# Moving gate products between three stages of a hybrid encoder block, with one convolution tap on ScalarE

## The chip, the cores and the metric

The kernel runs on one core of a Trainium2 chip. The time is that of the device in microseconds (us), median of repeated runs; a profile comes from one further execution. PE is TensorE (matmul), PEld its weight load, DVE VectorE, ACT ScalarE, POOL GpSimd, SP the queue that issues most DMAs.

## The reference

One layer of an encoder block over 1024 tokens of width 1024, in float32.

```python
h = rms_norm(x, norm1_w[l]) * (1.0 + scale1) + shift1
proj = h @ w_in[l]
q, k, v, xBC, z, dt_raw, gates = jnp.split(proj, offsets, axis=-1)
...
attn = block_attention(q, k, v)                    # 16 query heads of 64, 4 key/value heads, softmax over all tokens
ssd = ssd_mixer(xBC, z, dt_raw, ...)               # centred convolution of 5 taps, SiLU, chunked scan in both directions
g_attn = jax.nn.sigmoid(gates[..., :D_MODEL])
g_ssd = jax.nn.sigmoid(gates[..., D_MODEL:])
merged = g_attn * (attn @ w_attn_out[l]) + g_ssd * (ssd @ w_ssd_out[l])
x = x + gate1 * (merged @ w_o[l])
...
ff = jnp.square(jax.nn.relu(h2 @ w_mlp1[l])) @ w_mlp2[l]
x = x + gate2 * ff
```

The gates are 2048 columns of the input projection, 16 chunks of 128 columns. They are needed only after the scan, when the two branches are merged. The convolved columns xBC are 24 chunks.

## The kernel before

Every float32 matrix product is done as three: each operand is split into a high part (a cast on ACT) and a low part (a subtraction on DVE or POOL), and high x high, high x low and low x high are summed in PSUM. The function `split` at lines 168 to 170 does both steps, so all low parts are recorded under line 155 and all high casts under line 169.

The stages follow one another: modulation and norm; the projections for q, k, v and z; the convolved pairs (lines 704 to 843); attention (848 to 974); the scan (995 to 1206); the merge and the rest.

In the **convolved pairs** two chunks of 128 columns are projected together by seven block products instead of eight (a Winograd form of Strassen's scheme). The loop at line 802 goes over `pairs`. A pair loads its weights as `r0` and `r1` (`load_pair`; `r1` has one buffer), POOL forms four sums of weight blocks (`w_sum`), each product (`product`, 12 matmuls of 512 columns) takes an operand from one of four slots (`w1_op`), and DVE and POOL add the products into two padded rows `pa` and `pb`. For a convolved pair `conv` then runs five taps over each padded row: the first by a tensor_scalar on DVE at line 712, four more by scalar_tensor_tensor at 715, and SiLU on ACT at 717. Two pairs later at most, `to_tokens` turns the result by 16 transposes per pair. A gate pair is only written out. `GPOS` says at which places of the list gate pairs stand; with `(13,)` one gate pair stands last, and `GATES` = 14 chunks remain for direct products.

In **attention** a unit `u` is 128 queries of one head, 128 units in all: `scores(u)` (four matmuls), a maximum on DVE (line 893), the exponential on ACT (895), `turn` (eight transposes, then a split), and for each four units `values`, 16 matmuls. The sums of the exponentials are collected in `zall` and inverted only at the end (lines 965 to 969). Direct gate products run beside it: `weave` (line 64) takes the next step of the stream whose declared cost used so far is the smaller share of its declared total, so PE's order is written out by hand (`manual_schedule(engines=M2)`), 12 chunks at 10.4 beside 128 units at 2.72. A chunk is 2 halves of 24 matmuls. The other engines' order and the DMA queues' order are made by the planner from its own estimate of time.

In the **scan** the same weave runs `scan` beside `products`: the two remaining gate chunks, the attention's output product (8 chunks, with `load_a` reading outputs and reciprocals back, multiplying them on DVE and splitting them), and, once `pipe["done"]` has reached 16 scan chunks, the scan's output product. The tiles of the normed input `h` and of the read-back outputs `a` share one pool of 32 tiles (tag "act").

Of the kernel before, what the change touches and what calls it, by code (L numbers as in the profile page):

```python
# [9 lines left out]
F32 = mybir.dt.float32  # L10
# [8 lines left out]
P = 128  # L19
# [14 lines left out]
QKV_N = 400  # L34
GATES_EARLY = 12
LEAD2 = 0
# [7 lines left out]
NPRE = 5  # L44
GPOS = (13,)
KR = 4
# [45 lines left out]
def block(ctx: ExitStack, tc: tile.TileContext, ia, out, upto=99, dbg=None):  # L92
# [97 lines left out]

    def gemm_cm(ps_pool, tag, wsrcs, ahi, alo, evac, bufs=None, pair=False, then=None, e_lo=None):

        ws = {0: load_w(wsrcs[0], e_lo=e_lo)}
        if then:
            then()
        n = len(wsrcs)
        order = [(i, h) for i in range(n) for h in range(2)]
        if pair:
            order[:4] = [(0, 0), (1, 0), (0, 1), (1, 1)]
        for i, half in order:  # L200
            if half == 0 and i + 1 < n and i + 1 not in ws:
                ws[i + 1] = load_w(wsrcs[i + 1], e_lo=e_lo)
            hi, lo = ws[i]
            if 1:
                ps = ps_pool.tile([P, 512], F32, name=tag, tag=tag, bufs=bufs)
                for k in range(KT):
                    T.matmul(ps, hi[:, k], ahi[k][half], start=k == 0, stop=False)  # L207
                    T.matmul(ps, hi[:, k], alo[k][half], start=False, stop=False)  # L208
# [495 lines left out]
    with tc.tile_pool(name="p2", bufs=1, reuse_waits="tile") as p2, \  # L704
# [5 lines left out]
        def conv(i, pad):  # L710
            acc = accs.pop() if accs else acc_tile()
            V.tensor_scalar(out=acc, in0=pad[:, 0:S], scalar1=cwT[:, i:i + 1], scalar2=vecT[:, CB0 + i:CB0 + i + 1],
                            op0=ALU.mult, op1=ALU.add)
            for k in range(1, 5):
# [133 lines left out]
    with tc.tile_pool(name="p3k", bufs=1, reuse_waits="tile") as p3k, \  # L848
# [3 lines left out]
        def gates_stream(pool, psp, i0, i1, bufs=2, e_lo=None):  # L852
# [5 lines left out]
            yield from gemm_cm(psp, "psg", [w_cols(w_in, OFF_G + i * P) for i in range(i0, i1)], hhi, hlo, evac, bufs=bufs, e_lo=e_lo)  # L858

        def attn_stream():  # L860

# [47 lines left out]

            pvs = {}  # L910

            def values(b, hf):

                h = b // 2
                v1 = kv[h // 4][2]
                if hf == 0:
                    pvs[b] = ps3.tile([P, 512], F32, name="pv", tag="pv", bufs=1)
                pv, ph, pl = pvs[b], phs.pop((b, hf)), pls.pop((b, hf))
# [9 lines left out]
                if hf == 1:  # L928
                    ax = p3.tile([HD, 512], F32, name="ax", tag="ax", bufs=1)
                    A.copy(ax, pv[HD:])  # L930
                    av = p3.tile([HD, 512], F32, name="av", tag="av", bufs=2)
                    tt(V, av, ax, pv[:HD], ALU.add)
                    dma(av_d[h // 2][(h % 2) * HD:(h % 2 + 1) * HD, (b % 2) * 512:(b % 2 + 1) * 512], av)
                yield 0.92

# [13 lines left out]
            for u in range(NU + 4):  # L949
# [13 lines left out]
                if u % 4 == 3 and u < NU:  # L963
                    pvq = all_values(u // 4)
            ps = ps3.tile([P, 4, P], F32, name="pst", tag="pst", bufs=2)
            T.transpose(ps[:, 0], zall, ident)
            zt = p3.tile([P, P], F32, name="zt", tag="pf", bufs=2)
            V.reciprocal(zt, ps[:, 0])
            dma(rz_d.rearrange("h (a b) -> (h a) b", b=P), zt)

        with tc.manual_schedule(engines=M2):
            weave(tc, (attn_stream(), 128 * 2.72 + L0), (gates_stream(p3, ps3, 0, GATES_EARLY, 1, G), GATES_EARLY * 10.4), lead=LEAD2)
    if upto <= 3:
        return dict(gt_d=gt_d, av_d=av_d, rz_d=rz_d)


    def out_stream(ps_pool, tag, wsrcs, hi, lo, dst, pool, then, bufs=2):
        def evac(i, half, ps):
# [3 lines left out]

        yield from gemm_cm(ps_pool, tag, wsrcs, hi, lo, evac, bufs=bufs, pair=True, then=then)

# [10 lines left out]
    with tc.tile_pool(name="p4", bufs=1, reuse_waits="tile") as p4, \  # L995
# [712 lines left out]
```

## Time and profile before

| | |
|---|---|
| median of 3 runs | 2608.29 us (2607.74 to 2609.0) |
| profiled execution, its own time | 2610.79 us |
| its span, first to last instruction | 2608.8 us |
| mean granted TensorE clock | 0.975 |
| busy: PE, PEld, DVE, ACT, POOL | 93%, 74%, 71%, 42%, 39% |

Busy shares are means over stages with different limits, so the stages are read one at a time. Matmuls are pipelined: the time of one is longer than the distance to the next, and the distance is what counts. In a row of waits stand: engine, tile and line that waited, what released it, total us, times, longest us. In a row of groups stand: line, engine, operation, tiles, shapes and count; then busy us and mean ns; then idle us before them and who ended it.

### The profile page before, as it was taken

The numbers are of one execution on the slowest core, as the hardware profiler recorded it, in microseconds if no ns is written. First come the engines' busy times: TensorE is split into PE (matmuls) and PEld (weight loads), VectorE is DVE, ScalarE is ACT, GpSimd is POOL, SyncE is SP. The second block draws the span as 40 slices with busy tenths as digits, with TensorE's granted clock in tenths as the row PEclk, the third lists the DMA queues.
The fourth block names the chain that finished last, engine by engine and source line by source line (L and its number), as shares of the span: only waits on it lengthen the run. The fifth ranks groups of instructions, "written<-read, shape, count | busy, mean of one in ns | idle before, by whom it ended". The sixth has DMA issues, their size and how long they took to land.

```text
span 2608.8 us, 32331 instructions
## 1 busy us (share of the span) xinstructions
PE 2435.3 (93%) x11340; PEld 1940.2 (74%) x11340; DVE 1844.4 (71%) x2200; ACT 1105.0 (42%) x1928; POOL 1016.0 (39%) x728
## 2 busy tenths in 40 slices
PE   5999999998989999999799999998989999899995
PEld 5998777776767777777567767776777888688884
DVE  5756347888856666666487787546569888768889
ACT  5455422333346666666233444343332222364441
POOL 2310117766710000000155666424018866633356
PEclk9999999999999999999899999999999999899998
DMA  7653741323441212111866675466315544754432
GB/s 258 184 157 124 253 152 61 89 85 93 145 140 45 77 45 79 47 52 29 239 216 196 194 223 169 125 221 207 133 49 178 189 144 144 265 179 149 142 93 97
DMA packets 286788, 369.69 MB, mean 142 GB/s; under 512 B 34201, under 2 KB 167041, under 8 KB 286625
## 3 DMA queue, kind: packets, MB, share of 16 engines
q1 hardware_dynamic: 215297, 292.62, 36.3%
q10 hardware_dynamic: 71328, 74.99, 8.7%
q8 instruction: 90, 1.47, 0.2%
q14 instruction: 73, 0.60, 0.1%
HBM read 251.33 MB, written 116.20 MB: 141 GB/s over the span
## 4 chain that ended last, share of the span: by engine, by line
PE 67%; DVE 11%; DMA 8%; issue 6%; POOL 5%; ACT 2%; SPq 1%; DVEq 0%; ACTq 0%; POOLq 0%
PE pst L906 5%; PE pp L1313 4%; PE pp L1315 4%; PE pp L1314 4%; PE psq L381 4%; PE psq L382 4%; PE psq L380 4%; PE psg L207 3%; PE psg L208 3%; PE psg L209 3%; PE p L1655 3%; PE p L1656 3%; PE p L1654 3%; PE pss L889 2%; PE pss L891 2%
## 5 line engine op out<-in xcount | busy, mean ns | idle before, releaser
L893 DVE TENSOR_REDUCE nm<-pss 128x1 f32<-128x1024 f32 x128 | 156.6, 1224 | 140.1 <-PE pss L891 139.6
L381 PE MATMUL psq<-twl,hh 128*128 128x400 f32 (+1 forms) x512 | 192.9, 378 | 5.9 <-DVE twl L155 4.1
L1655 PE MATMUL p<-o,o 128*128 128x512 f32 x448 | 179.8, 401 | 19.1 <-DVE o L155 19.1
L380 PE MATMUL psq<-twh,hh 128*128 128x400 f32 (+1 forms) x512 | 192.2, 381 | 3.7 <-ACT qkvr L513 1.2
L382 PE MATMUL psq<-twh,hl 128*128 128x400 f32 (+1 forms) x512 | 191.8, 377 | 0.0
L155 DVE TENSOR_TENSOR pl<-pst,ph 128x512 fp32r<-128x512 f32 x256 | 168.4, 684 | 27.5 <-ACT ph L169 27.5
L1654 PE MATMUL p<-o,o 128*128 128x512 f32 x448 | 177.3, 399 | 9.6 <-ACT o L169 7.7
L895 ACT ACTIVATE pf<-pss,nm 128x1024 f32<-128x1024 f32 x128 | 142.8, 1115 | 101.6 <-PE pst L906 98.0
L155 POOL TENSOR_TENSOR wlo<-wraw,whi 128x1024 fp32r<-128x1024 f32 x12 | 28.7, 2390 | 399.0 <-ACT whi L169 358.3
L1656 PE MATMUL p<-o,o 128*128 128x512 f32 x448 | 177.0, 397 | 0.0
L169 ACT CAST ph<-pst 128x512 fp32r<-128x512 f32 x256 | 146.3, 585 | 51.7 <-PE pst L906 37.5
L906 PEld LDWEIGHTS pst<-masks,pf 128*128 128x128 f32 x1024 | 118.8, 140 | 66.2 <-issue 28.8
L906 PE MATMUL pst<-masks,pf 128*128 128x128 f32 x1024 | 157.0, 276 | 9.7 <-DVE pl L155 9.6
L155 POOL TENSOR_TENSOR sl<-sl 128x512 f32<-128x512 f32 x64 | 95.0, 1492 | 175.5 <-DVE o L155 83.2
L715 DVE SCALAR_TENSOR_TENSOR cacc<-pad,cwT,cacc 128x1024 f32<-128x1024 f32 x96 | 149.7, 1570 | 0.4
L169 ACT CAST o<-ar 128x512 fp32r<-128x512 f32 x112 | 69.8, 623 | 175.8 <-PE p L1656 155.2
L155 DVE TENSOR_TENSOR o<-ar,o 128x512 fp32r<-128x512 f32 x112 | 107.2, 957 | 48.1 <-ACT o L169 48.1
L169 ACT CAST wop<-ws 128x512 fp32r<-128x512 f32 x116 | 70.6, 620 | 122.7 <-PE pp L1315 69.2
L1655 PEld LDWEIGHTS p<-o,o 128*128 128x128 f32 x448 | 86.5, 193 | 41.6 <-DVE o L155 23.7
L381 PEld LDWEIGHTS psq<-twl,hh 128*128 128x128 f32 x512 | 98.5, 192 | 17.9 <-DVE twl L155 5.2
L155 DVE TENSOR_TENSOR o<-sl,o 128x512 fp32r<-128x512 f32 x112 | 111.3, 994 | 0.1
L380 PEld LDWEIGHTS psq<-twh,hh 128*128 128x128 f32 x512 | 98.0, 192 | 16.0 <-ACT qkvr L513 1.7
(416 smaller groups left out, 7166.0 us busy)
## 6 DMA issues: line engine op xcount, KB each, us to landing
ar<-r SPq DMA_DIRECT2D x112, 256.0 KB
wada<-in_w_ada_dram SPq DMA_DIRECT2D x48, 512.0 KB
r<-in_w_mlp_dram SPq DMA_DIRECT2D x32, 512.0 KB
r<-as SPq DMA_DIRECT2D x64, 256.0 KB
sl<-in_w_mlp_dram SPq DMA_DIRECT2D x64, 256.0 KB
r<-in_w_in_dram SPq DMA_DIRECT2D x26, 512.0 KB
r<-ro ACTq DMA_DIRECT2D x48, 256.0 KB
xb<-cst ACTq DMA_DIRECT2D x20, 512.0 KB
```

The lines of the kernel that those rows point to most:

```text
L155: e.tensor_tensor(out=o, in0=a, in1=b, op=op)
L169: (e_hi or A.copy)(hi, src)
L380: T.matmul(o, hhi[k][half][:, sl], hi[:, k % 2, :n], start=k == 0, stop=False)
L381: T.matmul(o, hhi[k][half][:, sl], lo[:, k % 2, :n], start=False, stop=False)
L382: T.matmul(o, hlo[k][half][:, sl], hi[:, k % 2, :n], start=False, stop=k == KT - 1)
L715: V.scalar_tensor_tensor(out=acc, in0=pad[:, k:k + S], scalar=cwT[:, 24 * k + i:24 * k + i + 1], in1=acc, op0=ALU.mult, op1=ALU.add)
L893: V.tensor_reduce(out=nm, in_=ps, axis=AX.X, op=ALU.max, negate=True)
L895: A.activation(pfs[u], ps, AF.Exp, bias=nm, accum_out=zall[:, u:u + 1])
L906: T.transpose(pt[:, k], pf[:, (hf * 4 + k) * P:(hf * 4 + k + 1) * P], ident)
L1654: T.matmul(pss[t], a[:, 0, sl], b[:, 0], start=k == 0, stop=False)
L1655: T.matmul(pss[t], a[:, 0, sl], b[:, 1], start=False, stop=False)
L1656: T.matmul(pss[t], a[:, 1, sl], b[:, 0], start=False, stop=k == KR - 1)
```

## The change

- `GPOS` becomes `(2, 5, 8, 11, 16)`: five gate pairs stand among the 17 pairs; six chunks remain for direct products, all of them in attention, none in the scan.
- In `conv` the first tap is an activation (Identity with scale and bias) on ScalarE.
- In `values` the reciprocals of a block of four units are formed on DVE, written to DRAM element by element, and read back broadcast over 64 partitions; POOL multiplies the output with them before it is written.
- A new `load_a` inside attention's second stream, behind the gates, loads and splits the first two weight chunks of the attention's output product and reads the outputs back, each two heads as soon as they are written.
- In the scan the product starts with what was loaded; the old `load_a` and the division there go.

```diff
-GATES_EARLY = 12
-GPOS = (13,)
+GPOS = (2, 5, 8, 11, 16)
...
-            V.tensor_scalar(out=acc, in0=pad[:, 0:S], scalar1=cwT[:, i:i + 1], scalar2=vecT[:, CB0 + i:CB0 + i + 1],
-                            op0=ALU.mult, op1=ALU.add)
+            A.activation(acc, pad[:, 0:S], AF.Identity, scale=cwT[:, i:i + 1], bias=vecT[:, CB0 + i:CB0 + i + 1])
...
+        heads = [0]
+        w_ahead = {}
+
+        def load_a():
+
+            hi, lo = act_tiles("a", KT)
+            for i in range(2):
+                w_ahead[i] = load_w(w_cols(w_ao, i * P), e_lo=G)
+            yield 2
+            for k in range(KT):
+                while heads[0] < 2 * k + 2:
+                    yield None
+                for half in range(2):
+                    raw = p3.tile([P, 512], F32, name="araw", tag="araw", bufs=2)
+                    dma(raw, av_d[k][:, half * 512:(half + 1) * 512])
+                    split(hi[k][half], lo[k][half], raw, e_lo=G)
+                yield 2
+            w_ahead["a"] = hi, lo
+
+        def beside():
+            yield from gates_stream(p3, ps3, 0, GATES, 1, G)
+            yield from load_a()
+
...
                 if hf == 0:
+                    zi = p3.tile([P, 4], F32, name="zi", tag="zi", bufs=2)
+                    V.reciprocal(zi, zall[:, 4 * b:4 * b + 4])
+                    row = rz_d[h:h + 1, (b % 2) * 512:(b % 2 + 1) * 512]
+                    dma(row.rearrange("a (t p) -> p (a t)", p=P), zi)
+                    rzs[b] = p3.tile([HD, 512], F32, name="rz", tag="rz", bufs=2)
+                    dma(rzs[b], rz_d[h, (b % 2) * 512:(b % 2 + 1) * 512].partition_broadcast(HD))
...
                     tt(V, av, ax, pv[:HD], ALU.add)
+                    tt(G, av, av, rzs.pop(b), ALU.mult)
                     dma(av_d[h // 2][(h % 2) * HD:(h % 2 + 1) * HD, (b % 2) * 512:(b % 2 + 1) * 512], av)
+                    heads[0] = (b + 1) // 2
...
-            ps = ps3.tile([P, 4, P], F32, name="pst", tag="pst", bufs=2)
-            T.transpose(ps[:, 0], zall, ident)
-            zt = p3.tile([P, P], F32, name="zt", tag="pf", bufs=2)
-            V.reciprocal(zt, ps[:, 0])
-            dma(rz_d.rearrange("h (a b) -> (h a) b", b=P), zt)
...
-            weave(tc, (attn_stream(), 128 * 2.72 + L0), (gates_stream(p3, ps3, 0, GATES_EARLY, 1, G), GATES_EARLY * 10.4), lead=LEAD2)
+            weave(tc, (attn_stream(), 128 * 2.72 + L0), (beside(), GATES * 10.4 + 18), lead=LEAD2)
...
-        ahi, alo = act_tiles("a", KT)
-
-        def load_a():
-            for half in range(2):
-                ns = slice(half * 512, (half + 1) * 512)
-                for k in range(KT):
-                    raw = p4.tile([P, 512], F32, name="araw", tag="araw", bufs=3)
-                    dma(raw, av_d[k][:, ns])
-                    rz = p4.tile([P, 512], F32, name="rz", tag="rz", bufs=2)
-                    for j in range(2):
-                        dma(rz[j * HD:(j + 1) * HD, :], rz_d[2 * k + j, ns].partition_broadcast(HD))
-                    tt(V, raw, raw, rz, ALU.mult)
-                    split(ahi[k][half], alo[k][half], raw)
-
+        ahi, alo = w_ahead.pop("a")
...
-            yield from gates_stream(p4, ps4, GATES_EARLY, GATES)
-            yield from out_stream(ps4, "psg", [w_cols(w_ao, i * P) for i in range(KT)], ahi, alo, a_d, p4, load_a)
+            yield from out_stream(ps4, "psg", [w_cols(w_ao, i * P) for i in range(KT)], ahi, alo, a_d, p4, ws=w_ahead)
...
-            weave(tc, (scan(), 32 * (5.54 + YC) + SC0 + 7 * SC1), (products(), 166.4 + (GATES - GATES_EARLY - HELD) * 10.4), lead=LEAD3)
+            weave(tc, (scan(), 32 * (5.54 + YC) + SC0 + 7 * SC1), (products(), 166.4 - HELD * 10.4), lead=LEAD3)
```

More of the change, by code (lines that the diff above doesn't have):

```diff
@@ L189, in w_cols, with gemm_cm @@
         return w[k0 * P:(k0 + KT) * P, c0:c0 + P].rearrange("(k p) c -> p k c", p=P)
-    def gemm_cm(ps_pool, tag, wsrcs, ahi, alo, evac, bufs=None, pair=False, then=None, e_lo=None):
-        ws = {0: load_w(wsrcs[0], e_lo=e_lo)}
+    def gemm_cm(ps_pool, tag, wsrcs, ahi, alo, evac, bufs=None, pair=False, then=None, e_lo=None, ws=None):
+        ws = ws or {0: load_w(wsrcs[0], e_lo=e_lo)}
         if then:
@@ L908, in turn @@
                 split(phs[b, hf][:, :, js], pls[b, hf][:, :, js], pt)
-            pvs = {}
+            pvs, rzs = {}, {}
             def values(b, hf):
@@ L964, in attn_stream, with out_stream @@
                     pvq = all_values(u // 4)
-            ps = ps3.tile([P, 4, P], F32, name="pst", tag="pst", bufs=2)
-            T.transpose(ps[:, 0], zall, ident)
-            zt = p3.tile([P, P], F32, name="zt", tag="pf", bufs=2)
-            V.reciprocal(zt, ps[:, 0])
-            dma(rz_d.rearrange("h (a b) -> (h a) b", b=P), zt)
         with tc.manual_schedule(engines=M2):
-            weave(tc, (attn_stream(), 128 * 2.72 + L0), (gates_stream(p3, ps3, 0, GATES_EARLY, 1, G), GATES_EARLY * 10.4), lead=LEAD2)
+            weave(tc, (attn_stream(), 128 * 2.72 + L0), (beside(), GATES * 10.4 + 18), lead=LEAD2)
     if upto <= 3:
         return dict(gt_d=gt_d, av_d=av_d, rz_d=rz_d)
-    def out_stream(ps_pool, tag, wsrcs, hi, lo, dst, pool, then, bufs=2):
+    def out_stream(ps_pool, tag, wsrcs, hi, lo, dst, pool, then=None, bufs=2, ws=None):
         def evac(i, half, ps):
@@ L981, in evac @@
             adma(dst[i][:, half * 512:(half + 1) * 512], st)
-        yield from gemm_cm(ps_pool, tag, wsrcs, hi, lo, evac, bufs=bufs, pair=True, then=then)
+        yield from gemm_cm(ps_pool, tag, wsrcs, hi, lo, evac, bufs=bufs, pair=True, then=then, ws=ws)
     def load_g(pool, k0, hi, lo):
```

## The prediction

> **What bounds the kernel now.** I read the page first, then busy time by windows, then in each touched stage the waits, the groups of instructions and the order of time. The change touches three stages: the convolved pairs (414 to 732 us), attention (about 741 to 1246) and the scan (1246 to 1716). The windows list PE, PE weight load, DVE, ACT and POOL busy time, then granted clock, DMA share and GB/s.
>
> ```profile
> span 2608.8 us, 32331 instructions
> ...
> 492.10:516.80 24.70, 21.63 (x102) 17.16 (x101) 20.83 (x19) 8.95 (x15) 17.48 (x15) 1.00 0.30 86
> 709.30:732.20 22.90, 19.26 (x84) 14.95 (x82) 18.73 (x17) 7.05 (x9) 12.13 (x11) 1.00 0.81 268
> 760.00:1240.00 480.00, 472.76 (x2499) 362.11 (x2498) 324.39 (x402) 316.74 (x557) 28.59 (x18) 1.00 0.19 54
> 1220.00:1240.00 20.00, 19.05 (x104) 14.51 (x103) 12.94 (x18) 12.79 (x24) 4.40 (x7) 1.00 0.07 20
> 1290.00:1300.00 10.00, 5.72 (x11) 2.91 (x11) 4.21 (x6) 2.76 (x4) 2.16 (x2) 0.52 1.05 271
> 1420.00:1440.00 20.00, 20.00 (x91) 14.38 (x90) 16.25 (x18) 7.59 (x16) 13.04 (x11) 1.00 0.66 197
> ```
>
> Attention is bound by PE (98.5% busy), and so is the scan after its first 70 us. The convolved pairs are not: a convolved pair takes 24.7 us, of which PE works 21.63. The waits between 438 and 709 us say what it lacks, and a piece of the chain of work through one pair says why.
>
> ```profile
> PE psc L770 <- DVE wop L155: 20.3, 10, 2.3
> PE psc L770 <- POOL wop L155: 6.4, 6, 2.4
> DVE cacc L712 <- POOL pad L155: 24.5, 11, 2.3
> ```
>
> ```profile
> 572.59 1.40 DMA r<-in_w_in_dram
> ...
> 576.46 2.00 POOL ws L155
> ...
> 585.42 1.06 POOL pad L155
> 586.51 1.58 DVE cacc L712
> ...
> 590.23 0.67 DVE pad L155
> ...
> 596.63 0.61 DVE wop L155
> ...
> 597.30 1.40 DMA r<-in_w_in_dram
> ```
>
> This is a loop of 24.7 us: the weights land (3.9 us), POOL forms its sums and the pad add (10.0 us), DVE works off convolution taps (from 586.5 on), and only then splits the low part of the fifth operand (596.63 to 597.24). That frees the single buffer for the next load, and PE stands 2.03 us before it. What PE would need alone comes from the order of time:
>
> ```profile
> 563.16 0.39 PE L768 MATMUL psc<-hh,wop 128*128 128x512 f32 x1
> 565.88 0.39 PE L768 MATMUL psc<-u2h,wop 128*128 128x512 f32 x1
> 573.17 0.63 PE L768 MATMUL psc<-u4h,wop 128*128 128x512 f32 x1
> 573.60 0.63 PE L769 MATMUL psc<-u4l,wop 128*128 128x512 f32 x1
> 576.31 1.03 PE L732 MATMUL pst<-masks,cacc 128*128 128x128 f32 x8
> ```
>
> Twelve matmuls lie between the first two starts, so one takes 2.72/12 = 0.227 us (0.43 us behind the 2 us gap, where the clock is lower). A pair has 7 products of 12 matmuls, 19.05 us; two convolved chunks add 16 transposes, 2.06 us. PE's floor is 21.1 us for a convolved pair and 19.05 for a gate pair.
>
> **The change part by part.** *Matmuls.* A gate chunk done directly is 2 halves x 24 = 48 matmuls; a pair done in seven products is 84 instead of 96. Four pairs move: 336 matmuls (+76.2 us) come into the convolved pairs, 6 x 48 = 288 (65.4 us) leave attention and 96 (21.8 us) leave the scan: 48 matmuls, 10.9 us fewer. The rest is decided by stalls.
>
> *Convolved pairs.* The first tap leaves DVE:
>
> ```profile
> L712 DVE TENSOR_SCALAR cacc<-pad,cwT,vecT 128x1024 f32<-128x1024 f32 x22 | 35.8, 1627 | 24.5 <-POOL pad L155 24.5
> L155 DVE TENSOR_TENSOR wop<-r,wop 128x512 fp32r<-128x512 f32 x33 | 32.0, 973 | 14.7 <-ACT wop L169 14.7
> L717 ACT ACTIVATE cacc<-cacc 128x1024 f32<-128x1024 f32 x22 | 23.4, 1061 | 130.3 <-DVE cacc L715 130.3
> ```
>
> Two taps of 1.63 us leave the DVE stretch of the loop and one ACT pass of 1.06 us enters it ahead of the first remaining tap (price by the SiLU row, the same shape on the same engine): 24.7 - 3.26 + 1.06 = 22.5 us. Behind a gate pair DVE has no backlog and the pair comes near PE's 21.1. As six convolved pairs follow a convolved one and six a gate pair or the start, I take 21.9 on average; the ends are 21.1 (PE) and 24.7 (nothing gained). ACT's time is covered: 8.95 us busy of 24.7, and 2.1 more. A gate pair in the middle keeps 5 pad adds and 3 low splits on DVE, about 6.3 us, but inherits the taps in front of it; I take 20.0 (ends 19.05 and 22.9, the last gate pair now). Now: 12 x 24.7 + 21.5 = 318 us. After: 12 x 21.9 + 4 x 20.0 + 21.5 = 364. **+46 us**, ends +33 and +92.
>
> On the port the Trainium skill has a rule (SBUF — State Buffer, Who interferes with whom): a DVE instruction in a two-port mode, or with two SBUF inputs, and a GpSimd instruction reading SBUF lock each other out, and ScalarE never waits. The tap's 1.63 us would then be time taken from POOL as well, and the pairs would reach PE's floor, 10 us better; the sum keeps POOL's 10.0 us as measured.
>
> *Attention.* First the score tiles' instructions (count, least, median and longest ns, first and last start), then groups between 760 and 1240 us, PE's own wait there, and the third load of queries in SP's queue:
>
> ```profile
> L893 DVE TENSOR_REDUCE nm<-pss x128: 1214/1225/1226, 742.4 to 1230.9; 128x1 f32<-128x1024 f32 x128
> ...
> L895 ACT ACTIVATE pf<-pss,nm x128: 1113/1115/1126, 743.6 to 1234.1; 128x1024 f32<-128x1024 f32 x128
> L895 ACT ACTIVATION_READ_ACCUMULATOR pf<-pss,nm x128: 188/192/209, 744.6 to 1235.1; 128x1 f32 x128
> ```
>
> ```profile
> L155 DVE TENSOR_TENSOR pl<-pst,ph 128x512 fp32r<-128x512 f32 x248 | 163.1, 684 | 27.5 <-ACT ph L169 27.5
> L169 ACT CAST ph<-pst 128x512 fp32r<-128x512 f32 x249 | 142.6, 585 | 51.2 <-PE pst L906 36.9 <-PE pv L925 13.4
> L155 DVE TENSOR_TENSOR av<-ax,pv 64x512 f32<-64x512 f32 x31 | 21.0, 677 | 4.9 <-ACT ax L930 4.9
> L169 ACT CAST whi<-wraw 128x1024 fp32r<-128x1024 f32 x11 | 11.6, 1052 | 2.5 <-PE psg L208 2.5
> ```
>
> ```profile
> PE pst L906 <- DVE pl L155: 9.6, 17, 1.6
> ```
>
> ```profile
> 763.54 0.32 SPq L874 DMA_DIRECT2D q<-q  x1
> ```
>
> A unit (128 queries of a head) takes (1230.9 - 742.4)/127 = 3.85 us, 1.02 of it the 4.5 gate matmuls woven in; 2.83 remain. The weave shares PE by the costs that the code declares: six chunks are 62.4 of 80.4, so they are used up at 78% of attention, unit 98. Until there a unit holds 2.94 gate matmuls: 2.83 + 0.67 = 3.50 us. The last 30 units have no gate work, and then the engines are nearly level: PE 2.83; DVE 1.225 + 2 x 0.684 + a quarter of an output add (about 0.17) + a small reciprocal, 2.85; ACT 1.115 + 0.192 + 2 x 0.585 + a quarter of an output copy (0.15), and a thirtieth of sixteen read-back casts and two weight casts of 1.05, 3.01; copies and casts of 512 columns at the 0.585 of the cast shown. I take 3.2, since hand-overs now already cost PE 0.95 us in 20 (window 1220 to 1240). 98 x 3.50 + 30 x 3.2 = 439 against 492: **-53 us**; ends -59 (3.01) and -39 (3.55 and 3.5).
>
> What else is added there: 32 reciprocals and 32 products with them on POOL, which is busy 28.6 us of 480; 32 element-wise writes and 32 broadcast reads on SP. These stand in SP's queue ahead of the output writes and next head's queries. Head 2's queries are now asked for at 763.5 us and first used at unit 16, 742.4 + 16 x 3.85 = 804, so a write and a read of 4.8 us each (row below) ahead of them are hidden; without that cover PE would wait at 14 heads, at most 9.6 us each. Elements of 4 bytes are not in this trace; were a write ten times 4.8 us, it would pass the 40 us.
>
> *Scan.* The two gates (21.8 us) go, and with them the 48 loads, 16 products and 32 splits that started it:
>
> ```profile
> PE psg L207 <- ACT ah L169: 8.4, 3, 4.3
> PE pst L1032 <- POOL xdb L155: 5.5, 1, 5.5
> ...
> PE psg L208 <- DVE al L155: 2.6, 2, 2.1
> ```
>
> ```profile
> 1259.98 4.80 DMA rz<-rz
> ```
>
> ```profile
> L155 POOL TENSOR_TENSOR pad<-pad,p x26: 1082/1092/1100, 437.8 to 732.1; 128x512 f32<-128x512 f32 x26
> ```
>
> Those waits of PE are 16.5 us, the second because DMA is saturated (share 1.05); lower clock behind them costs some 3 more. I credit 15 (ends 11 and 20). New is a wait at the front: the last head's output is copied and added (0.59 + 0.68), multiplied on POOL (1.1), written and read back (4.8 each), and split (0.59 + 1.1) before the eighth step of the first product: 13.7 us after PE's last attention matmul. Seven steps cover 7 x 3 x 0.227 = 4.8: 9 us as it stands, less where a DMA is quicker than in that crowded stretch; I take 8 (ends 3 and 13). And the first output product now ends at 83.2/145.6 = 57% of the weave, where the scan has written 13 chunks; the second may start at 16. For about 2.3 chunks the scan runs alone, at DVE's pace of 12.5 x 16.25/20 = 10.2 us for 7.24 us of PE work (the declared cost): 6 us idle. Sum: -21.8 - 15 + 8 + 6 = **-23 us**, ends -36 and -10.
>
> Later stages keep their work. The sum is 46 - 53 - 23 = -30 us against the profiled execution's 2610.8 us (span 2608.8, 2.0 around it). The median of the runs, 2608.3, is 2.5 lower, so the forecast is 2608.3 - 30 = **2578 us**, 1.2% faster.
>
> **The rivals.** (A) *The loop stays*: another item in it, POOL's sums or the load, takes the place of the taps and a convolved pair stays at 24.7. Then +34 more: 2612, no change. For it: POOL is busy 17.5 of 24.7 us and PE already waits for its splits (6.4 us). Against: the loop is one chain, and two of its links go.
>
> (B) *Attention without filler is bound by its softmax chain*: units fall to 3.6 us and no further. -31 instead of -53: 2600. For it: PE's idle 9.6 us in attention is all behind DVE's low split. Against: these waits are a fiftieth of the stage.
>
> (C) *Slower: the tap blocks ScalarE's queue.* It waits for the pad, as DVE's did, 24.5/11 = 2.2 us; behind it stand the casts that start every operand. A tap held 2.2 + 1.1 us that PE does not cover makes a pair 21.9 + 3.3 = 25.2: +40, **2618 us**. It decides from 24.9 us a convolved pair on, where the sum passes +5. For it: seven casts a pair share that queue. Against: four operand slots let casts run ahead, and ACT idles 15 us a pair.
>
> (D) *The clock falls in the last 30 units*: if short gaps brought the 0.43 us matmul there, a unit would cost 2.83 more: +85, 2663. Against: in 1220 to 1240 us, with such gaps, the granted clock is 1.00; only gaps of 2 us lowered it. The Trainium skill (TensorE: Matmul & The Clock Gate, A second HAM failure mode: psum-queue depth-cycling) says frequent micro-idles between groups can make the clock oscillate; the traced window does not agree.
>
> (E) *All stalls go*: pairs at PE's floor, attention and scan at their good ends: 33 - 59 - 36 = -62, 2546.
>
> **How the numbers follow.** Forecast 0.56 (own range 2558 to 2597), A 0.12, B 0.11, C 0.11, D 0.03, E 0.07. About 0.2% (5.2 us) is what a measurement of this kernel tells from no change. Faster: forecast, E, most of B and a little of A, 0.75; same: most of A, 0.11; slower: C, D, 0.14. The range, 2546 to 2613, reaches from E to A and leaves out C and D and the far side of E.
>
> **What would show it.** Right: convolved pairs about 22 us apart with PE no longer waiting for the fifth operand's low split; score reductions 3.5 us apart up to unit 98 and about 3.2 behind it; the products' first matmuls at the scan's start with one wait for the eighth step. Wrong: pairs still 24.7 apart (A), 3.6 us units early on (B), casts idle behind the tap on ACT (C), a granted clock under 1 late in attention (D). A changed order of instructions in later stages, which I count at nothing, would move the sum without any of these.

## The result

| | median | range, runs | ratio to before, 95% interval |
|---|---|---|---|
| before | 2608.29 us | 2607.74 to 2613.32, 5 | |
| after | 2636.18 us | 2623.55 to 2639.59, 5 | 1.0094, 1.0067 to 1.012 |

The change makes the kernel 0.9% slower; the forecast was 1.2% faster. Three rows place the difference. The first two are from the page of the kernel after, the third from its view of the score tiles (count; least, median and longest ns; first and last start in us).

```profile
span 2630.4 us, 32563 instructions
...
PE 2427.9 (92%) x11291; PEld 1933.0 (73%) x11291; DVE 1851.1 (70%) x2203; ACT 1135.3 (43%) x1964; POOL 1119.9 (43%) x828
```

```profile
L914 DVE TENSOR_REDUCE nm<-pss x128: 1214/1224/1227, 791.5 to 1288.5; 128x1 f32<-128x1024 f32 x128
```

The first score maximum ends what lies before attention, the last one ends attention but for its tail. With the span, every run falls into three parts that add up to it:

| us | up to the first maximum | first to last maximum | behind it | span |
|---|---|---|---|---|
| before | 742.4 | 488.5 | 1377.9 | 2608.8 |
| after | 791.5 | 497.0 | 1341.9 | 2630.4 |
| difference | +49.1 | +8.5 | -36.0 | +21.6 |
| forecast | +46 | -53 | -23 | -30 |

The profiled execution of the kernel after is 4 us shorter than its median (2632.16 against 2636.18), so the spans differ by 21.6 us where the medians differ by 27.9.

The convolved pairs are as forecast, the scan is 13 better, and the whole miss is attention: 61.5 us. PE has less work there than before and stands more. These are the waits of three engines between 790 and 1301 us after (SP's row is its queue's):

```profile
SPq L943 <- DMA rz<-zi: 276.4, 31, 10.7
```

```profile
ACT ah L168 <- DMA araw<-av: 29.8, 6, 7.2
```

```profile
PE pst L927 <- DVE pl L154: 59.6, 66, 5.8
PE psg L206 <- ACT ost L853: 4.0, 1, 4.0
```

PE's wait for DVE's low split was 9.6 us and 17 times before; now it is 59.6 and 66 times. Two things are in it. Seven units take 5.6 to 10.7 us from one maximum to the next, where no unit of before takes over 5; the other 120 take 3.67 on average, so the seven are together 31 us longer than seven of the others. First one of the long units, in the chain of waits (start, us, what) and in the order of time (the last bracket is the idle time before the instruction and what ended it):

```profile
1160.55 0.18 DVE zi L939
1160.74 8.44 DMA rz<-zi
1169.20 0.46 SPq L943
...
1169.78 4.00 DMA av<-av
1173.80 0.04 issue
1173.85 2.78 DMA araw<-av
...
1177.17 0.58 ACT ph L168
1177.75 1.12 ACT pf L916 x2
```

```profile
1166.53 1.29 POOL L154 TENSOR_TENSOR av<-av,rz 64x512 f32<-64x512 f32 x1 [13.99 <-DVE av L154]
...
1169.78 0.51 SPq L961 DMA_DIRECT2D av<-av  x1
...
1176.65 0.62 ACT L168 CAST ah<-araw 128x512 fp32r<-128x512 f32 x1 [4.00 <-DMA araw<-av]
...
1177.65 1.12 ACT L916 ACTIVATE pf<-pss,nm 128x1024 f32<-128x1024 f32 x1
```

The write of the reciprocals, 512 elements of 4 bytes, takes 8.44 us. SP's next item is the broadcast read of what is written, so SP stands until 1169.20, and the output write behind it, whose product POOL has ready at 1167.82, goes at 1169.78. It takes 4.00, the read-back 2.78, and the read-back's cast, which the planner has put ahead of the next exponential in ScalarE's order, waits idle for 4.00 us. The exponentials and high casts of attention stand behind it, and with them DVE's low split and PE. The Trainium skill (PSUM — Partial Sum Buffer, Engine vs sequencer instructions) says that ScalarE's queue is strictly first in, first out; these rows agree.

Between the long units the chain of waits shows a circle that closes in 3.56 us, here among the last units, without a gate matmul:

```profile
1200.12 1.22 DVE nm L914
1201.34 0.61 DVE pl L154
1201.95 0.14 issue
1202.08 0.63 PE pst L927 x4
1202.71 0.46 PE pss L910 x2
1203.17 0.48 PE pss L912 x2
1203.66 0.02 issue
1203.68 0.87 DVE nm L914
```

DVE takes the next unit's maximum ahead of this unit's low split. The turned tile has two slots in PSUM; PE's next turn waits for the slot that the low split reads, the scores stand behind that turn in PE's order, and the next maximum behind the scores. The second of two windows (PE, PEld, DVE, ACT, POOL, then granted clock, DMA share, GB/s) holds these units: PE is busy for 16.17 us of 20 at full clock. The first holds two long units:

```profile
1158.00:1200.00 42.00, 31.72 (x165) 23.42 (x164) 24.34 (x33) 24.46 (x43) 7.49 (x5) 0.96 0.23 70
1200.00:1220.00 20.00, 16.17 (x90) 11.63 (x89) 15.48 (x21) 13.61 (x26) 2.56 (x2) 1.00 0.06 14
```

### The profile page after: what moved, and what is told of

Its sections match the earlier page's. It is cut to its first block, busy times and chain, and to the rows that moved or that the text cites. A ratio compares the mean times of both kernels' runs of the same rounds, so it can differ in the third digit from the quotient of the medians.

```text
span 2630.4 us, 32563 instructions
## 1 busy us (share of the span) xinstructions
PE 2427.9 (92%) x11291; PEld 1933.0 (73%) x11291; DVE 1851.1 (70%) x2203; ACT 1135.3 (43%) x1964; POOL 1119.9 (43%) x828
## 4 chain that ended last, share of the span: by engine, by line
PE 38%; DMA 8%; DVE 6%; issue 3%; POOL 2%; ACT 1%; SPq 0%; DVEq 0%; ACTq 0%; POOLq 0%
PE pp L1323 4%; PE pp L1325 4%; PE pp L1324 4%; PE p L1665 3%; PE p L1666 3%; PE p L1664 3%; DMA rz<-zi 2%; PE psy L1150 2%; PE psg L206 2%; PE pso L1124 2%; DVE o L154 2%; PE psg L207 2%; PE psg L208 2%; DVE ac L154 1%; PE pso L1370 1%
## 5 line engine op out<-in xcount | busy, mean ns | idle before, releaser
L927 PE MATMUL pst<-masks,pf 128*128 128x128 f32 x1024 | 161.6, 281 | 59.7 <-DVE pl L154 59.6
L154 POOL TENSOR_TENSOR av<-av,rz 64x512 f32<-64x512 f32 x32 | 41.0, 1282 | 339.9 <-DVE av L154 332.7
L713 DVE SCALAR_TENSOR_TENSOR cacc<-pad,cwT,cacc 128x1024 f32<-128x1024 f32 x96 | 159.5, 1691 | 0.4
L168 ACT CAST wop<-ws 128x512 fp32r<-128x512 f32 x132 | 81.5, 622 | 130.6 <-PE pp L1325 69.3
L154 POOL TENSOR_TENSOR wop<-ws,wop 128x512 fp32r<-128x512 f32 x68 | 121.5, 1800 | 20.8 <-ACT wop L168 20.6
L154 DVE TENSOR_TENSOR wop<-r,wop 128x512 fp32r<-128x512 f32 x89 | 97.7, 1098 | 20.5 <-ACT wop L168 20.2
```

The lines of the kernel that those rows point to most:

```text
L154: e.tensor_tensor(out=o, in0=a, in1=b, op=op)
L168: (e_hi or A.copy)(hi, src)
L713: V.scalar_tensor_tensor(out=acc, in0=pad[:, k:k + S], scalar=cwT[:, 24 * k + i:24 * k + i + 1], in1=acc, op0=ALU.mult, op1=ALU.add)
L927: T.transpose(pt[:, k], pf[:, (hf * 4 + k) * P:(hf * 4 + k + 1) * P], ident)
```

## The experiments

Every ratio is to runs of the kernel before on the same chip. "Start", "attention" and "behind" are the three parts of the table above, from the span and the score tiles' row of each run.

| run | median us | ratio, 95% interval | start | attention | behind |
|---|---|---|---|---|---|
| e1_pool_cast | 2600.22 | 0.9962, 0.995 to 0.9974 | 791.8 | 464.6 | 1339.7 |
| e2_no_div | 2595.03 | 0.994, 0.9924 to 0.9957 | 789.9 | 465.8 | 1338.7 |
| e3_dve_tap | 2653.39 | 1.016, 1.0141 to 1.0178 | 809.0 | 501.0 | 1344.2 |
| e4_half_max | 2579.62 | 0.9877, 0.9862 to 0.9892 | 788.1 | 440.5 | 1343.5 |
| e5_tap_only | 2600.82 | 0.9966, 0.9955 to 0.9977 | 727.1 | 488.6 | 1387.9 |
| e6_four_pairs | 2601.33 | 0.9958, 0.9943 to 0.9974 | 775.4 | 475.2 | 1343.1 |
| e7_seven_pairs | 2624.87 | 1.0053, 1.0034 to 1.0072 | 827.0 | 454.5 | 1342.3 |
| e8_dve_by_hand | 2651.27 | 1.0153, 1.0135 to 1.0172 | 793.0 | 489.7 | 1372.2 |
| e9_scores_later | 2625.14 | 1.0053, 1.0037 to 1.007 | 791.3 | 488.5 | 1342.2 |
| e10_turns_first | 2698.04 | 1.0332, 1.0317 to 1.0348 | 793.4 | 564.1 | 1343.4 |
| e11_plain_write | 2601.45 | 0.9961, 0.9947 to 0.9976 | 790.4 | 466.3 | 1341.8 |
| e12_free_slot | 2716.77 | 1.0404, 1.0387 to 1.042 | 789.4 | 578.7 | 1345.7 |
| e13_low_from_sbuf | 2565.8 | 0.9828, 0.9814 to 0.9843 | 789.3 | 422.3 | 1353.6 |
| e14_three_slots | 2610.08 | 1.0, 0.9989 to 1.0012 | 844.8 | 405.2 | 1356.8 |
| e15_row_write | 2570.41 | 0.9837, 0.9822 to 0.9853 | 843.8 | 383.9 | 1344.2 |

### The long units

**e1_pool_cast** is the changed kernel with the read-back's casts on GpSimd:

```diff
-                    split(hi[k][half], lo[k][half], raw, e_lo=G)
+                    split(hi[k][half], lo[k][half], raw, e_hi=G.tensor_copy, e_lo=G)
```

> The changed kernel, but the high casts of the outputs read back in attention are on POOL instead of ScalarE. Theory 1 (the read-back stalls attention because its casts stand in ScalarE's queue and wait there for their DMA, with the exponentials behind them; the eight long units of the changed profile are 33 us longer than the others): 2636 - 33 = 2603 us, and no unit over 5 us. Theory 2 (the units are long because the division's round trip holds the output tiles, whatever casts them): no change, 2630 to 2640. Under both, ordinary units without gate work stay at 3.56 us.

**e2_no_div** takes the reciprocals, their write and read and the product out of attention, and leaves the casts on ScalarE:

```diff
-                    zi = p3.tile([P, 4], F32, name="zi", tag="zi", bufs=2)
-                    V.reciprocal(zi, zall[:, 4 * b:4 * b + 4])
...
-                    tt(G, av, av, rzs.pop(b), ALU.mult)
```

> The changed kernel without the division inside attention: no reciprocals, no write and read of them, no product on POOL (the output is left undivided, so the result lacks the softmax's sum); the read-back stays, with its casts on ScalarE. If the element-wise write (8.5 us in the changed profile, 32 times, with SP's queue standing behind it) is what makes the outputs and so the casts late: the long units shrink by most of their 33 us, 2605 us. If the read itself, its own trip behind the output's write of 4 us, is late enough: about 10 us at most, 2625. If neither matters: 2636.

Each alone takes all long units away: attention 464.6 and 465.8 against 497.0. In the run with the casts on GpSimd no ScalarE instruction waits for a read-back any more, and PE's wait for the low split is

```profile
PE pst L927 <- DVE pl L154: 38.6, 62, 1.5
```

with 1.5 us as the longest, 5.8 in the changed kernel. So the casts in ScalarE's order and the division's chain are needed together; 32 us hang on the pair.

**e11_plain_write** tells whether the chain as such or the length of its first link does it:

```diff
-                    dma(row.rearrange("a (t p) -> p (a t)", p=P), zi)
+                    dma(row.rearrange("a (p t) -> p (a t)", p=P), zi)
```

> The changed kernel, its casts on ScalarE, with the write of the inverse sums put down in the order in which they lie in SBUF: four neighbouring elements of a partition together, 128 pieces of 16 bytes in place of 512 of 4. The sums then stand at other places in the row, so the division is by other columns' sums; the work is otherwise the same. Theory that the length of this write (8.5 us) makes the long units: the write takes 4 us or less, as the others do, each of the eight long units gets shorter by some 3 to 4.5 us (33 us of extra becomes 0 to 10), attention 497 to 468-478, time about 2608-2615. If the long units come from the order of the casts in ScalarE's queue whatever the write takes: 2630-2636.

Attention falls to 466.3, the rest of the code as it was. The wait of SP for that write, and ScalarE's for the read-back, between 790 and 1269 us:

```profile
SPq L943 <- DMA rz<-zi: 41.2, 32, 3.1
```

```profile
ACT ah L168 <- DMA araw<-av: 3.7, 4, 1.1
```

With pieces of 16 bytes SP stands 41.2/32 = 1.3 us per write, with pieces of 4 bytes 276.4/31 = 8.9. As long as the casts stand on ScalarE, the length of this write makes the long units, and 30.7 us of attention are its price. The Trainium skill (DMA: Bandwidth & Descriptors, Specifications) puts the smallest transfer at line rate at 512 bytes; both sizes lie far below.

### The floor of a unit

**e4_half_max** takes e1 and lets DVE's maximum read half the columns:

> As the kernel with the casts on POOL, but the softmax's maximum goes over 512 of the 1024 scores of a row (about 0.66 instead of 1.22 us on DVE; the queries are scaled by 0.01 so that nothing overflows, which leaves out nothing in time): the result is another. If the unit of 3.56 us is a chain through DVE, where the next maximum stands between two low splits and PE's next transposes wait for the second: units without gate work fall by about 0.5 us to 3.0 to 3.1, attention becomes bound by PE at about 3.3 on average, 30 to 40 us below the kernel with the casts on POOL. If the unit is bound by ScalarE or by the hand-overs alone: no change against it.

The maximum takes 0.692 us in place of 1.225, and attention falls by 24.1 us, 0.19 for each unit:

```profile
L914 DVE TENSOR_REDUCE nm<-pss x128: 680/692/694, 788.1 to 1228.6; 128x1 f32<-128x512 f32 x128
```

The maximum is in the circle, but only a third of what it lost came out as time (a half in the sixteen last units, 3.31 us each in place of 3.57). It doesn't tell whether the slot closes the circle or the softmax chain itself. Three runs tried to open it by another order of the work, and a fourth by a copy.

**e8_dve_by_hand** keeps DVE in the order of the program (`M2` gets DVE beside PE), which takes the low split of a unit first:

> The changed kernel with the read-back's casts on GpSimd, and VectorE's order in attention as the program writes it instead of the planner's. Theory that the floor of a unit is made by VectorE taking the next unit's maximum ahead of the low part of this unit's split: the units without gates fall below 3.57 us, toward 3.0 to 3.3, attention 464.6 to 430-445, time about 2565-2580. If the order only moves the wait to another place (the maximum then comes late for the exponentials), no gain or a loss: 2600 or more.

It is slower. DVE now stands in its own order:

```profile
DVE pl L154 <- ACT ph L168: 155.5, 66, 12.4
```

In most blocks the four units take about 4.3, 2.9, 5.5 and 2.3 us. The low split is now taken first and DVE stands for ScalarE's cast ahead of it, time in which the other order has the next maximum done. That is the second theory's loss, though by another wait than the one it names. Behind attention 32 us more than in e1 are spent as well; why was not followed.

**e9_scores_later** gives the scores of the unit after next behind the first turn:

> The changed kernel with the read-back's casts on GpSimd (2600.22 alone), and the scores of the unit after next given to TensorE behind the first of this unit's two turns instead of ahead of both. Theory that the floor of 3.56 is the circle maximum, low part of the split, turn, scores, maximum: the two turns that wait for a low part then stand together and the scores no longer stand behind only one of them; if that opens the circle, units toward 3.2 to 3.4 and 2565 to 2590. If the circle only closes in another order (the second turn of one unit and the first of the next both wait for the same maximum's successors), no change, 2595 to 2610, or slower by what a second waiting turn adds (0.6 a unit, 2670).

**e10_turns_first** gives both turns first, then the scores, then the values:

```diff
-                if u + 2 < NU:
-                    scores(u + 2)
-                    yield 0.92
                 for hf in range(2):
                     if u < NU:
                         turn(u, hf)
                         yield 0.44
-                    if hf == 0:
-                        c = next(pvq, None)
-                        if c:
-                            yield c
+                if u + 2 < NU:
+                    scores(u + 2)
+                    yield 0.92
+                c = next(pvq, None)
+                if c:
+                    yield c
```

> The changed kernel with the read-back's casts on GpSimd, and TensorE's order in a unit changed to both turns, then the scores of the unit after next, then the values' matmuls. The values' 1.9 us then stand between the scores and the next waiting turn, and cover the maximum (1.22) and the low parts (1.26) that follow the scores. If the floor is that circle: units of TensorE's own work and less than half of the present waits (0.6 to 0.7 us per unit in the run with the casts on GpSimd), 3.0 to 3.3, attention 385 to 430, time 2525 to 2570. If the wait for the exponential or for a slot of the turned tile takes its place: 2595 or more.

Both are slower than e1, by 25 and 98 us. PE's wait in e10 (790 to 1370 us):

```profile
PE pst L927 <- DVE pl L154: 117.6, 91, 2.8
```

Two turns in a row need both slots at once, and PE stands for a low split 91 times where e1 has 62. That speaks for the slot, not yet against the chain.

**e12_free_slot** copies the turned tile out of PSUM and splits it from SBUF:

```diff
-                split(phs[b, hf][:, :, js], pls[b, hf][:, :, js], pt)
+                pr = p3.tile([P, 4, P], F32, name="pr", tag="pr", bufs=2)
+                A.copy(pr, pt)
+                split(phs[b, hf][:, :, js], pls[b, hf][:, :, js], pr, e_hi=G.tensor_copy)
```

> The changed kernel with the read-back's casts on GpSimd (2600.22 alone), and the turned tile copied whole out of PSUM by ScalarE; the high part is then cast by GpSimd from that copy and the low part formed by VectorE from it, both from SBUF, so that the PSUM slot comes free with ScalarE's copy and not with VectorE's low part (to make room in SBUF the read-back has one raw tile in place of two, and so has the gates' result). Theory that the floor of 3.56 is a circle through the slot (maximum, low part, turn, scores, maximum): the low part drops out of it and VectorE may be late; units of 2.9 (TensorE's work beside no gate) to 3.25, attention 464.6 to 385-420, time 2520-2560. Rival, that the floor is VectorE's and ScalarE's chain of the softmax as such (maximum, exponential, turn, cast): GpSimd's cast (0.61) comes into the chain as one more step and the units stay or grow: 2600-2640. Should GpSimd and VectorE slow one another on SBUF, VectorE's low parts take longer than 0.68 each and the units 3.4 or more: 2580-2610.

The slowest run, and no test of the slot: the two buffers of the copy took the place of the two slots, and GpSimd's cast came into the same circle as a further link. One row of its waits (790 to 1370 us):

```profile
ACT pr L930 <- DVE pl L154: 146.8, 99, 7.8
```

**e13_low_from_sbuf** takes the slot out of the circle and leaves every instruction in number and size:

```diff
-                split(phs[b, hf][:, :, js], pls[b, hf][:, :, js], pt)
+                A.copy(phs[b, hf][:, :, js], pt)
+                tt(V, pls[b, hf][:, :, js], masks[:, 0:4], phs[b, hf][:, :, js].bitcast(F32), ALU.subtract)
```

> The changed kernel with the read-back's casts on GpSimd (2600.22 alone), and the low part of the split formed as a constant in SBUF less the high part, in place of the turned tile in PSUM less the high part: the same instruction in number and size, it still waits for ScalarE's cast, but the slot of the turned tile is free once that cast is done. The low parts then hold other values, so the attention output is another; nothing else is left out. If the floor is the circle through the slot: the wait of TensorE's turns for low parts goes, units of 2.9 to 3.3 us, attention 464.6 to 385-425, time 2520 to 2562. If the floor is the softmax chain as such (maximum, exponential, turn, cast): no change, 2595 to 2605.

Attention 422.3, 42.3 us less than e1, and PE's wait for the low split is gone from its waits (790 to 1229 us, the first three rows):

```profile
PE pv L950 <- DVE av L154: 15.8, 10, 4.8
PE pst L927 <- ACT ph L929: 2.2, 4, 0.9
PE pss L910 <- ACT pf L916: 1.6, 1, 1.6
```

The slot was the floor. The low split itself is as long as it was (a median of 683 ns, 681 in e1), and the softmax chain, with the same maximum, exponential, turn and cast, goes at 422.3/127 = 3.33 us a unit, gates included. Of the 42.3 us 13.9 are lost again behind attention, where PE stands 4.8 us for the last output add and 7.0 for the read-back's cast (0.9 and 3.8 in e1); that is half of it, and the rest was not followed.

**e14_three_slots** gives the turned tile a third slot, in the bank that is free when no gate is left in attention:

```diff
-GPOS = (2, 5, 8, 11, 16)
+GPOS = (1, 3, 5, 8, 10, 13, 15, 18)
...
-                pt = ps3.tile([P, 4, P], F32, name="pst", tag="pst", bufs=2)
+                pt = ps3.tile([P, 4, P], F32, name="pst", tag="pst", bufs=3)
```

> The changed kernel with the read-back's casts on GpSimd, all eight gate pairs among the convolved pairs and none in attention, and in the PSUM bank that the gates' results leave free a third slot for the turned tile. The pairs cost three times 17 us more by the run with seven of them: 366.7 to 417-422. If the floor is the circle through the slot: units fall below 3.57, toward 2.9 to 3.3, attention 370 to 420 where seven pairs and two slots had 454.5, time 2560 to 2605. If it is the softmax chain as such: attention 452 to 455, time 2638 to 2650.

Attention 405.2, where seven pairs and two slots had 454.5; the middle unit takes 2.74 us. PE's waits (845 to 1270 us, the first two rows) have little left for the slot:

```profile
PE pv L950 <- DVE av L154: 40.5, 12, 8.3
PE pst L928 <- DVE pl L154: 10.4, 10, 2.5
```

The pairs give 53 us back (start 844.8), so the time is that of before, 5 us above the range that was expected for the slot. Nine units over 5 us have come back.

**e15_row_write** turns the sums into rows on TensorE before the write, so that it goes out in four pieces of 512 bytes:

```diff
-                    zi = p3.tile([P, 4], F32, name="zi", tag="zi", bufs=2)
-                    V.reciprocal(zi, zall[:, 4 * b:4 * b + 4])
+                    zp = ps3.tile([P, 4, P], F32, name="pst", tag="pst", bufs=3)
+                    T.transpose(zp[0:4, 0], zall[:, 4 * b:4 * b + 4], ident)
+                    zi = p3.tile([4, P], F32, name="zi", tag="zi", bufs=2)
+                    V.reciprocal(zi, zp[0:4, 0])
...
-                    dma(row.rearrange("a (t p) -> p (a t)", p=P), zi)
+                    dma(row.rearrange("a (t p) -> (a t) p", p=P), zi)
```

> The run with three slots and no gates in attention (2610.08, attention 405.2), and the sums of a block turned by TensorE from four columns to four rows before the reciprocal, so that the write of the inverse sums is four pieces of 512 bytes in place of 512 of 4 bytes; it takes one slot of the turned tile once per block. Theory that the long units there (38 us over nine) come from the 8.5 us write, which holds up the reciprocal and GpSimd's multiplication: the write falls to some 4 us or less, long units go, attention 405 to 362-378, time 2567 to 2583. If they come from the queues as such: 2600 to 2612.

Attention falls by another 21.3 us, less than the 27 to 43 expected, and 12.6 come from behind it, where PE's waits for the last output add and for the read-back's high cast fall from 8.3 and 7.7 us to 1.6 and none; one unit over 5 us is left, the second of all. The turn of the sums has a price: PE stands 24.1 us in 30 waits until the reciprocal has read its slot. SP's wait for the write (830 to 1230 us), and the engines' busy time in attention (columns as above):

```profile
SPq L946 <- DMA rz<-zi: 21.8, 16, 2.8
```

```profile
850.00:1200.00 350.00, 327.77 (x1875) 256.50 (x1874) 319.25 (x404) 270.81 (x492) 59.69 (x54) 1.00 0.22 61
```

This version computes what the reference does and beats both kernels: 1.6% under the kernel before. PE and DVE are both near full in it, 94% and 91%.

### Gates and the tap

**e3_dve_tap** puts the first tap back on VectorE in the changed kernel; **e5_tap_only** is the kernel before with the tap on ScalarE and nothing else. This is the edit of e5; e3's is its reverse.

```diff
-            V.tensor_scalar(out=acc, in0=pad[:, 0:S], scalar1=cwT[:, i:i + 1], scalar2=vecT[:, CB0 + i:CB0 + i + 1],
-                            op0=ALU.mult, op1=ALU.add)
+            A.activation(acc, pad[:, 0:S], AF.Identity, scale=cwT[:, i:i + 1], bias=vecT[:, CB0 + i:CB0 + i + 1])
```

> The changed kernel with the first convolution tap back on DVE. By the prediction's loop (two taps of 1.63 us in DVE's stretch, 1.25 us of ScalarE instead) the twelve convolved pairs grow by about 2 us each, 20 to 30 us in all: 2656 to 2666. If gate pairs between the convolved ones already relieve DVE enough, the tap is worth nothing: 2636.

> The kernel before with one part of the change alone: the first tap of each convolved pair as an activation on ScalarE. Theory of the prediction (the pair is bound by VectorE's queue and gets shorter by 2.8 us less what ScalarE gives back, 24.7 to 21.9): 17 pairs without a gate part gain 2.2 to 2.8 each, stretch of the pairs 314 to about 270-275, time about 2570. Theory from the run with the tap put back on VectorE (17 us for 12 to 14 pairs without a gate part, 1.2 to 1.4 each): 314 to 288-294, time about 2585-2590. If the tap only helps beside the gate parts of the changed kernel: 2605-2610.

The start moves from 809.0 to 791.5 by the tap in the changed kernel, 17.5 us, and from 742.4 to 727.1 in the kernel before, 15.3: 1.3 to 1.5 us for each of 12 convolved pairs (the 17 pairs that e5's text counts are those of the changed kernel). From the first product of the first pair to that of the last, e5 is 19.3 us shorter than before; pairs in a row start 22.7 us apart in place of 24.7, but the first three gain only 0.7 us together. Its first product starts 3.9 us later, which takes the rest; that start lies between 412 and 418 us in eleven of the runs, with the tap on either engine. Of e5's 15.3 only 9.4 are left in its median; its profiled run is 10.0 longer behind attention, where its code is that of before. Why, no run tells. What is left of PE's waits for the fifth operand in the changed kernel (440 to 770 us), and the tap itself beside the SiLU row:

```profile
PE psc L768 <- DVE wop L154: 8.7, 6, 2.3
PE psc L768 <- POOL wop L154: 1.6, 1, 1.6
```

```profile
L711 ACT ACTIVATE cacc<-pad,vecT,cwT x24: 1243/1246/1253, 440.8 to 766.9; 128x1024 f32<-128x1024 f32 x24
L715 ACT ACTIVATE cacc<-cacc x24: 1057/1062/1066, 454.5 to 781.4; 128x1024 f32<-128x1024 f32 x24
```

**e6_four_pairs** and **e7_seven_pairs** are e1 with `GPOS = (3, 7, 11, 15)` and `(1, 3, 6, 9, 12, 15, 18)`, so eight and two gate chunks in attention.

> The changed kernel with the read-back's casts on GpSimd, and four gate pairs among the convolved pairs in place of five, so eight gate chunks in attention in place of six. Theory that the units have a floor of 3.56 us whatever is beside them, and that those with gates lie a little above it: attention 464.6 to about 470-475, convolved pairs 366.7 to about 347, time about 2585-2590. Theory of the prediction that TensorE's work sets attention (a gate chunk costs all of its 10.9 us): attention about 486, pairs 347, time about 2602.

> The changed kernel with the read-back's casts on GpSimd, and seven gate pairs among the convolved pairs, so two gate chunks in attention. Floor theory: attention 127 units of 3.56 to 3.58 us, 452 to 455, pairs 366.7 to about 407, time about 2625-2630. Theory of the prediction (TensorE's work sets attention): attention 464.6 less 43.6, 421, pairs 407, time about 2593-2597.

Attention is as the floor theory has it, 475.2 and 454.5. The time of e7 is too; that of e6, 2601.33, is the other theory's, though its profiled execution is 2595.51. A gate pair costs 16.4 to 17.6 us at the start. Out of attention it saves 10.6 between eight chunks and six (475.2 to 464.6), and only 5.05 between six and two (464.6 to 454.5, two pairs). PE's own 21.8 us a pair are not saved: a unit with nothing beside it still takes its 3.56, and the gate matmuls lay in its gaps. Moving gates out of attention costs more than it brings as long as the floor stands.

## Why the prediction was wrong

*Convolved pairs, +46: right (+49.1), from two misses that cancel.* Four gate pairs cost 809.0 - 742.4 = 66.6 us, 16.7 each where I took 20.0, less than PE's own 19.05. In e3 PE idles no more with 17 pairs than before with 13 (29.1 us between 438 and 809, 31.0 between 438 and 742), at a clock of 0.98 in place of 0.96; what else spares time there was not separated. The tap brought 17.5 us, not 12 x 2.8 = 33.6. It takes 1.246 us, not the 1.06 of the SiLU row. The loop's 22.5 us were near, 22.7 in e5; the average over all pairs was not, as the first ones gain next to nothing. The text also counts six pairs behind a convolved one and six behind a gate pair or the start; by `GPOS` they are seven and five, which leaves its 21.9 as it is. Rival C doesn't happen: the pairs in a row got shorter with the tap on ScalarE.

*Attention, -53: wrong (+8.5).* Two steps of the prediction failed.

The first is "a thirtieth of sixteen read-back casts": I counted these casts by their length and not by what they wait for. The text asked what the new DMAs stand ahead of in SP's queue and found the queries' load, which is indeed covered; it didn't ask what waits for their end. That is a cast in ScalarE's order, ahead of an exponential. I took 4.8 us for the element-wise write and saw a danger only at "ten times 4.8 us"; it takes 8.4 us, far under that, and still cost 31 to 32 us of attention, as e11, e1 and e2 each show by another way.

The second is "98 x 3.50 + 30 x 3.2": I took a unit to be worth the engines' work in it. Rival B had the right number, 3.6 us and no further, and the row for it, PE's waits behind DVE's low split; I put it at 0.11 because these waits were a fiftieth of the stage. They were few because the gate matmuls, 4.5 a unit, filled the circle's gap. By e1, without the write's stalls, attention is 23.9 us better than before (488.5 to 464.6), near B's 31. Of the 29 us that are missing, 18 lie in the first 98 units (3.68 us each in e1, 3.50 forecast) and 11 in the others (3.57, 3.2 forecast); PE stands for a low split in both. B's reason was not exact: e13 and e14 show that it is not the softmax chain but the two slots of the turned tile. With the slot out of the circle the units take 3.33 with gates, and with three slots and no gates the middle one takes 2.74; I had added up 2.83 to 3.01 for the engines. The sum of engine work was sound, and what stood above it was a buffer.

The two together: 32.4 (e1) + 29.1 (464.6 - 488.5 = -23.9 in place of -53) = 61.5 us, the whole miss of the stage.

*Scan, -23: somewhat better (-36.0 behind the last maximum).* All of it is in the scan: its second output product starts 253.9 us behind the last maximum, 292.0 before. The 8 us at its front for the last read-back came out small: PE stands there once, 3.3 us, where it stood 8.4 in three waits before, and without any division (e2) only 3.2 us less is spent behind attention. The wait for POOL that I credited as gone (5.5 us) is still there, 8.1 us. The forecast's ends for this stage, -36 and -10, are wider than the ends named for its terms, which with the 6 us held fixed give -33 and -14.

*Rivals.* A and E don't occur. D: the clock is 1.00 in the last units, with gaps of some 0.7 us every 3.56; around two long units it is 0.96, and over all of attention 0.97 where e1 has 1.00, so a lower clock has a part in the 32 us; how large a part was not separated. No rival had a wait on ScalarE for the read-back.

## What to carry to other kernels

A cast that reads what a DMA brings can hold its engine for what is left of the DMA's whole chain; when that engine is on the critical path, give such work to one that may wait, and shorten the chain's first link. Writing elements of 4 bytes across partitions is what to look for: turning them into rows first brought some 40 us from e14 to e15 (2610.08 to 2570.41), with PE's 24.1 us of waits for it included.

A stage that looks bound by an engine may run on a circle through a buffer, whose gaps are filled by other work. Before taking that work away, add up the circle (who frees the slot, what stands behind the waiting instruction): here the gaps stayed when the filler went, and another slot was then worth more than less work (454.5 to 405.2 us of attention, where four gate chunks fewer had brought 10.1).

## What the runs showed of the hardware

- A write of 128 x 4 float32 from SBUF to DRAM: 8.44 us in 512 pieces of 4 bytes; in 128 pieces of 16 bytes SP stands 1.3 us for it on average, and in four pieces of 512 bytes 21.8/16 = 1.4 us on the occasions when it stands at all.
- ScalarE's Identity with a scale and a bias per partition takes 1.246 us on 128x1024 from one tile into another; SiLU in place 1.062.
- The middle unit of attention takes 2.74 us with three PSUM slots for the turned tile and no gates (e14). With two slots the sixteen last units, which have no gates beside them either, take 3.57 on average in e1, e6 and e7.
